# Squares of the tokens summed by ScalarE from a second, token-major load, and the in-projection's first two token tiles taken through the weights together

## The chip, the cores and the metric

One core of one Trainium2 chip runs the whole program. The metric is the device time of one execution in microseconds (us), the median of several runs.

## What is computed

The reference is one layer of a bidirectional encoder on two requests of 2048 and 256 tokens, in float32. The change lies in the first step of it, the normalized input projection of the attention heads and gates:

```
def rmsnorm(x, w):
    y = x * rsqrt(mean(x * x, axis=-1) + EPS)
    return y * w
...
h = rmsnorm(x, norm1_w)
p = h @ w_in            # split into mLSTM q,k,v,o; gates; attention q,k,v
m_out = mlstm_mixer(...)      # both directions, chunks of 64
a_out = attention_mixer(...)  # per-head RMS norm of q and k, rotary angles, softmax
x = x + concat(m_out, a_out) @ w_out
x = x + (silu(g) * a) @ w_down   # [a; g] = depthwise conv of rmsnorm(x) @ w_up
```

After it a final RMS norm. Each token has 1024 channels; the mean of their squares gives one factor `rc` per token.

## The kernel before

The 2304 tokens are 18 tiles of 128; tiles 16 and 17 are the short request and come first, then tiles 0 to 15 (`order`). A float32 product is made of three matmuls on split operands: a value is a rounded high part and a low remainder, and high·high, high·low and low·high are added (L260). `phase_a` handles the columns of `w_in` for attention and gates, 800 of them; the mLSTM's part, attention, out-projection and feed-forward follow later and are not touched.

For tile i of `phase_a`:

- `front_a` (L189) loads x channel-major: 128 channels on the partitions, 8 groups of channels by 128 tokens, 512 KB, into a buffer `x` (three of them; tiles 16 and 17 use buffers named `first`).
- `front_b` makes the high part on ScalarE (L196) and the low part on VectorE (L197) into `n1T` (three buffers) and stores both, 1 MB, for the later phases (L198).
- `front_c` squares x on ScalarE (L205, output `xq`), and GpSimd adds the 8 channel groups in three steps, 512, 256 and 128 elements per partition (L208 twice, L209, output `sq`).
- `front_d` sums the remaining 128 channels with a matmul against ones (L216, `rs_a`), adds EPS on VectorE (L218) and takes the power -1/2 on GpSimd (L219), which gives column i of `rc`.
- `mm` (L260) makes the projection `pj`: 8 chunks c of channels, two ranges of columns (512 and 288), three matmuls each, 48 matmuls per tile. Two `pj` buffers exist. Weights `w_a` are loaded and split per chunk in `weights` (L111, L112, L116).
- `post_a` scales `pj` by `rc` on ScalarE into `qk` (L269; two buffers), splits v, adds the gate bias (`gtm`, L278), squares q and k (L281), sums per head (`ms`, L283), and GpSimd makes the factors `rqk` (L104, L105).
- `post_b` on VectorE multiplies by `rqk` (L289), applies the rotary tables `tab` (L298, L302, L304) and splits into `kz` and `qz` (ScalarE L308, VectorE L309).
- `post2` transposes `kz` on TensorE (`pk`, L344) and stores it. `pg` (L337) are transposes of gates.

The rotary tables are multiplied with the head-norm weights once: two tiles' worth on VectorE and 28 small products on GpSimd (`tables2`, L247). During the first 8 tiles the weights of the mLSTM (`rm`, `wm`) are also loaded and split.

Each engine takes its instructions strictly in the order of its own stream. That order comes from a scheduler of the program's framework, which places instructions by priorities and a model of their times; a moved statement can so shift neighbours. DMAs issued from SyncE stand in SyncE's stream in the same way, so that one that waits for a free buffer holds those behind it.

Of the kernel before, what the change touches and what calls it, by code (L numbers as in the profile page):

```python
# [9 lines left out]
F32 = mybir.dt.float32  # L10
F32R = mybir.dt.float32r
AF = mybir.ActivationFunctionType
ALU = mybir.AluOpType
# [4 lines left out]
P = 128  # L18
D = 1024
NCC = D // P  # L20
T1, T2 = 2048, 256
T = T1 + T2
NT = T // P
# [4 lines left out]
EPS = 1e-6  # L28
# [125 lines left out]
def phase_a(g, tc, sw, st_x, after_x, after_mm, after_pj, wm):  # L154


    nc = g.nc
    with ExitStack() as st:
# [21 lines left out]
        xw = [first[k].rearrange("p (c t) -> p c t", c=NCC) for k in range(NX0)]  # L180

        xs = {}
        sqs = {}

        def front_a(i):

# [13 lines left out]

        def front_c(i):

            x = xs.pop(i)
            xq = sx.tile([P, NCC, P], F32, tag="xq", name=f"xq{i}", bufs=2)
            nc.scalar.activation(xq, x, AF.Square, scale=1.0 / 32.0)  # L205
            sq = sf.tile([P, P], F32, tag="sq", name=f"sq{i}")
            for k in (4, 2):
                nc.gpsimd.tensor_tensor(xq[:, 0:k], xq[:, 0:k], xq[:, k:2 * k], ALU.add)  # L208
            nc.gpsimd.tensor_tensor(sq, xq[:, 0], xq[:, 1], ALU.add)  # L209
            sqs[i] = sq  # L210

        def front_d(i):

            sq = sqs.pop(i)
            ps = pp.tile([P, 2], F32, tag="rs", name=f"rs_a{i}", bufs=2)
            nc.tensor.matmul(ps, sq, g.ones, start=True, stop=True)  # L216
            r = g.rc[:, i:i + 1]
            nc.vector.tensor_scalar(r, ps[:, 0:1], EPS, None, ALU.add)  # L218
            nc.gpsimd.tensor_tensor(r, r, g.mhalf[:, 0:1], ALU.pow)  # L219

        def weights(cs):
            for c in cs:
                r = first[NX0 + c] if NX0 + c < 8 else sx.tile([P, D], F32, tag="x", name=f"ra{c}", bufs=3)
                split(g, ws[c][:, 0, :], ws[c][:, 1, :], g.w_a[c], r[:, 0:800], g.n1w[:, c:c + 1])
# [25 lines left out]
        def mm(*tiles):  # L250

            pjs = [pj_.tile([P, 1024], F32, tag="pj", name=f"pj{i}", bufs=2) for i in tiles]
            cols = ((0, 512), (512, 800))
            if tiles[0] == order[0]:
                steps = [(t, z, c) for c in range(NCC) for t in range(len(tiles)) for z in cols]
            else:
                steps = [(0, z, c) for z in cols for c in range(NCC)]
            for t, (c0, c1), c in steps:
                for k, (a, b) in enumerate(((0, 0), (0, 1), (1, 0))):
                    nc.tensor.matmul(pjs[t][:, c0:c1], nTs[tiles[t]][:, c, a, :], ws[c][:, b, c0:c1],  # L260
                                     start=(c == 0 and k == 0), stop=(c == NCC - 1 and k == 2))
            for i in tiles:
                nTs.pop(i)
            return pjs
# [82 lines left out]

        front_a(order[0])
        front_b(order[0])
        weights(range(0, 3))  # L350
        front_a(order[1])
        front_c(order[0])
        weights(range(3, 6))
        front_b(order[1])
        front_a(order[2])
        weights(range(6, NCC))
        front_c(order[1])
        front_b(order[2])
        tables()
        front_d(order[0])  # L360
        front_c(order[2])
        tables2(slice(0, 2))
        front_a(order[3])
        prev = []
        steps = []
        for n, i in enumerate(order):
            pj, = mm(i)
            if n + 1 < NT:
                front_d(order[n + 1])
            if n > 1:  # L370
                post2(order[n - 2], prev.pop(0))
            if n == NT - 1:
# [1400 lines left out]
def layout(inputs):  # L1773
# [4 lines left out]
    def col(v):  # L1778
# [4 lines left out]
    w_m = np.concatenate([w_m[:LASTP], w_m[LASTP:][:, :, :, [1, 2, 0, 3]]], axis=0)  # L1783
    arrays = {
        "xT": x.reshape(NT, P, NCC, P).transpose(0, 3, 2, 1),
        "w_a": np.concatenate([w_in[:, ACOL + 32:ACOL + 800], w_in[:, ACOL:ACOL + 32]], axis=1).reshape(NCC, P, 800),
        "w_m": w_m.reshape(4, NCC, P, 512),
        "w_up": inputs["w_up"][0].reshape(NCC, P, 2 * NFC, P).transpose(2, 1, 0, 3),
# [26 lines left out]
```

## Time and profile before

| | us |
|---|---|
| median of 3 runs | 3365.33 (3363.44 to 3370.14) |
| the profiled execution | 3363.86 |
| its span in the trace | 3361.9 |
| TensorE busy in the span | 3262.6 |
| in-projection of `phase_a`, first to last matmul | 8.2 to about 205 |

The profile is one execution on the chip. Engines are PE (TensorE; PEld its weight loads), DVE (VectorE), ACT (ScalarE), POOL (GpSimd) and SP (SyncE). L12 is line 12 of the kernel; busy time excludes waiting. A row of the timeline gives start, duration, engine, line, operation, output and inputs, how many instructions were merged, and in brackets the idle time ahead of it with what ended it. A row of the table by stretches gives a stretch of the span, its length, the busy time and number of instructions of each engine, the clock granted to TensorE (1.00 is full), the mean busy share of the 16 DMA engines, and what they moved in GB/s.

### The profile page before, as it was taken

The numbers are of one execution on the slowest core, as the hardware profiler recorded it, in microseconds if no ns is written. First come the engines' busy times: TensorE is split into PE (matmuls) and PEld (weight loads), VectorE is DVE, ScalarE is ACT, GpSimd is POOL, SyncE is SP. The second block draws the span as 40 slices with busy tenths as digits, with TensorE's granted clock in tenths as the row PEclk, the third lists the DMA queues.
The fourth block names the chain that finished last, engine by engine and source line by source line (L and its number), as shares of the span: only waits on it lengthen the run. The fifth ranks groups of instructions, "written<-read, shape, count | busy, mean of one in ns | idle before, by whom it ended". The sixth has DMA issues, their size and how long they took to land. (4 is left out here: it accounts for less than half of the span.)

```text
span 3361.9 us, 57158 instructions
## 1 busy us (share of the span) xinstructions
PE 3262.6 (97%) x21366; PEld 3038.9 (90%) x21366; DVE 2399.9 (71%) x3721; ACT 1803.6 (54%) x3799; POOL 1355.2 (40%) x1710
## 2 busy tenths in 40 slices
PE   8899999999999999899999999999999999999998
PEld 6788888888888888788888999999999998999998
DVE  7866687777768778976765778978877776453573
ACT  5546666667666777655553544446555555323331
POOL 8653033213333323421245457744544442751112
PEclk9999999999999999999999999999999999999999
DMA  8665333343336444433347334424232223875563
GB/s 273 224 202 165 94 118 106 99 129 94 118 105 190 131 134 127 124 111 96 99 141 262 116 109 141 146 88 177 100 100 94 94 100 110 303 259 173 174 217 105
DMA packets 300636, 483.03 MB, mean 144 GB/s; under 512 B 36597, under 2 KB 186279, under 8 KB 300359
## 3 DMA queue, kind: packets, MB, share of 16 engines
q1 hardware_dynamic: 247543, 348.34, 32.7%
q0 software_dynamic: 36256, 121.60, 10.9%
q10 hardware_dynamic: 16560, 9.44, 0.9%
q8 instruction: 168, 2.75, 0.3%
q14 instruction: 109, 0.89, 0.1%
HBM read 337.37 MB, written 141.91 MB: 143 GB/s over the span
## 5 line engine op out<-in xcount | busy, mean ns | idle before, releaser
L634 DVE TENSOR_TENSOR pl<-ps,ph 128x512 fp32r<-128x512 f32 x520 | 353.9, 684 | 206.8 <-ACT ps L633 194.8
L1238 PE MATMUL pa<-nt,wut 128*128 128x290 f32 (+1 forms) x3168 | 447.0, 297 | 7.8 <-ACT u L1256 5.7
L632 ACT ACTIVATE ph<-ps 128x512 fp32r<-128x512 f32 x520 | 309.8, 596 | 248.7 <-PE ps L629 243.3
L1238 PEld LDWEIGHTS pa<-nt,wut 128*128 128x128 f32 x3168 | 431.1, 189 | 10.3 <-ACT u L1256 7.8
L603 DVE TENSOR_REDUCE mx<-px 128x1 f32<-128x512 f32 (+1 forms) x528 | 346.3, 673 | 94.3 <-PE px L602 92.2
L1348 DVE SCALAR_TENSOR_TENSOR y<-u,cw,y 128x1152 f32<-128x1152 f32 (+1 forms) x176 | 319.1, 1813 | 38.3 <-ACT yc L1346 17.3
L646 PE MATMUL pv<-ph,v 128*128 128x512 f32 (+1 forms) x1040 | 318.8, 401 | 0.8 <-ACT ph L632 0.3
L633 ACT ACTIVATE ps<-ps 128x512 f32<-128x512 f32 x520 | 310.2, 597 | 0.0
L1567 PE MATMUL et<-tet,wet 128*128 128x384 f32 x1584 | 279.0, 336 | 0.0
L1567 PEld LDWEIGHTS et<-tet,wet 128*128 128x128 f32 x1584 | 277.1, 188 | 0.0
L1081 PEld LDWEIGHTS po<-cmx,wo 128*128 128x128 f32 x1728 | 222.3, 192 | 9.7 <-DVE cmx L1069 1.5
L1081 PE MATMUL po<-cmx,wo 128*128 128x256 f32 x1728 | 226.4, 285 | 1.5 <-DVE cmx L1069 1.3
L1567 PE MATMUL e<-te,we 128*128 128x384 f32 x1188 | 213.5, 340 | 13.1 <-ACT te L1409 7.1
L1567 PEld LDWEIGHTS e<-te,we 128*128 128x128 f32 x1188 | 210.7, 190 | 14.5 <-ACT te L1409 7.3
L628 PE MATMUL ps<-qq,kk 128*128 128x512 f32 x520 | 214.9, 415 | 4.6 <-DVE mx L603 2.8
L602 PE MATMUL px<-kk,qq 128*128 128x512 f32 (+1 forms) x528 | 203.0, 412 | 4.1 <-DVE mx L603 2.4
L629 PE MATMUL ps<-qm,kl 65*128 65x512 f32 x520 | 205.9, 398 | 0.0
L792 PE MATMUL mj<-mn,wm 128*128 128x256 f32 x1296 | 197.9, 287 | 5.4 <-ACT og L808 3.4
L792 PEld LDWEIGHTS mj<-mn,wm 128*128 128x128 f32 x1296 | 182.7, 191 | 21.6 <-ACT og L808 3.8
L802 PEld LDWEIGHTS mv<-wm,mn 128*128 128x128 f32 x1296 | 183.1, 190 | 18.0 <-ACT qb L798 1.9
L802 PE MATMUL mv<-wm,mn 128*128 128x256 f32 x1296 | 196.9, 285 | 1.2 <-ACT qb L798 1.1
L646 PE MATMUL pv<-pl,v 128*128 128x512 f32 x520 | 191.6, 400 | 0.1
(310 smaller groups left out, 7244.9 us busy)
## 6 DMA issues: line engine op xcount, KB each, us to landing
mn<-n_d SPq DMA_DIRECT2D x216, 256.0 KB, 3.2
ru<-w_up SPq DMA_DIRECT2D x88, 512.0 KB, 3.6
a_d<-y POOLq DMA_DIRECT2D x88, 288.0 KB, 2.6
a_d<-tc POOLq DMA_DIRECT2D x66, 288.0 KB, 2.9
n_d<-n1T SPq DMA_DIRECT2D x18, 1024.0 KB, 5.3
dm<-nm_d POOLq DMA_DIRECT2D x72, 256.0 KB, 4.1
mjn<-n_d SPq DMA_DIRECT2D x72, 256.0 KB, 3.6
mvn<-n_d SPq DMA_DIRECT2D x72, 256.0 KB, 3.1
```

What stands on the lines that cost most here:

```text
L603: nc.vector.tensor_reduce(s.mx[:, t, z0:z0 + 1], ps[:, 0:w], AX.X, ALU.max)
L628: nc.tensor.matmul(ps, kk[:, kc:kc + P], s.qq[:, 0:N], start=True, stop=False)
L632: nc.scalar.activation(ph, ps, AF.Exp)
L633: nc.scalar.activation(ps, ps, AF.Exp)
L634: nc.vector.tensor_tensor(pl, ps, f32(ph), ALU.subtract)
L646: nc.tensor.matmul(s.pv[0:HD if k in (1, 3) else P, 0:N], v, p, start=(kp == 0 and k == 0), stop=(2 * kp + 2 == s.nk and k == 5))
L792: nc.tensor.matmul(pj[:, o], s.w[c][:, a, o * P:(o + 1) * P], nT[c][:, :, h, :], start=(c + o + k == 0), stop=(c == NCC - 1 and k == 2 and ...
L802: nc.tensor.matmul(pv[:, o], nT[c][:, o, a, :], s.w[c][:, h, 256:512], start=(c + o + k == 0), stop=(c == NCC - 1 and k == 2 and o == 1))
L1081: nc.tensor.matmul(po[:, o], wo[z // 2][c][:, a, n], mx[c][:, h, :], start=(c == 0 and k == 0), stop=(c == NCC - 1 and k == 2))
L1238: nc.tensor.matmul(p[:, z], w[:, aa, c, :], ops[k][:, c, bb, z * m:z * m + m], start=c == 0 and i == 0 and not add, stop=c == NCC // 2 - 1 ...
L1348: nc.vector.scalar_tensor_tensor(y[:, s:e], u[:, s + k:e + k], cw[:, k, jj:jj + 1], y[:, s:e], ALU.mult, ALU.add)
L1567: nc.tensor.matmul(ps[m // 2][:, m % 2], w[:, aa, m * P:(m + 1) * P], t[:, bb], start=p == 0 and n == 0, stop=p == NP - 1 and n == 2)
```

## The change

`front_c` no longer takes the channel-major x. It loads the tile once more from a second copy of the tokens, `xtok`, that lies token-major in memory (128 tokens on the partitions, 1024 channels, 512 KB), squares it on ScalarE and lets the same instruction add up the row, so that the sum lands directly in column i of `rc`; GpSimd adds EPS and takes the power. The three GpSimd additions, the matmul against ones and VectorE's addition of EPS are gone, and `front_d` with them. The copy is made on the host by a reshape of the input.

The first call of `mm` now takes tiles 16 and 17 together: chunk by chunk, with tile 17 two chunks behind tile 16. The loads at the start change order with it: one weight chunk, then x of tile 17, then the other weights.

```diff
         def front_c(i):
-            x = xs.pop(i)
-            xq = sx.tile([P, NCC, P], F32, tag="xq", name=f"xq{i}", bufs=2)
-            nc.scalar.activation(xq, x, AF.Square, scale=1.0 / 32.0)
-            sq = sf.tile([P, P], F32, tag="sq", name=f"sq{i}")
-            for k in (4, 2):
-                nc.gpsimd.tensor_tensor(xq[:, 0:k], xq[:, 0:k], xq[:, k:2 * k], ALU.add)
-            nc.gpsimd.tensor_tensor(sq, xq[:, 0], xq[:, 1], ALU.add)
-            sqs[i] = sq
-
-        def front_d(i):
-            sq = sqs.pop(i)
-            ps = pp.tile([P, 2], F32, tag="rs", name=f"rs_a{i}", bufs=2)
-            nc.tensor.matmul(ps, sq, g.ones, start=True, stop=True)
+            xs.pop(i)
+            xq = sx.tile([P, D], F32, tag="xq", name=f"xq{i}", bufs=2)
+            nc.sync.dma_start(xq, g.xtok[i])
             r = g.rc[:, i:i + 1]
-            nc.vector.tensor_scalar(r, ps[:, 0:1], EPS, None, ALU.add)
+            nc.scalar.activation(xq, xq, AF.Square, scale=1.0 / 32.0, accum_out=r)
+            nc.gpsimd.tensor_scalar(r, r, EPS, None, ALU.add)
             nc.gpsimd.tensor_tensor(r, r, g.mhalf[:, 0:1], ALU.pow)
...
             if tiles[0] == order[0]:
-                steps = [(t, z, c) for c in range(NCC) for t in range(len(tiles)) for z in cols]
+                steps = [(t, z, n - 2 * t) for n in range(NCC + 2) for t in range(2) if 0 <= n - 2 * t < NCC for z in cols]
...
         front_a(order[0])
         front_b(order[0])
-        weights(range(0, 3))
+        weights(range(0, 1))
         front_a(order[1])
-        front_c(order[0])
+        weights(range(1, 3))
+        front_b(order[1])
         weights(range(3, 6))
-        front_b(order[1])
         front_a(order[2])
         weights(range(6, NCC))
+        front_c(order[0])
+        front_b(order[2])
         front_c(order[1])
-        front_b(order[2])
         tables()
-        front_d(order[0])
         front_c(order[2])
...
-            pj, = mm(i)
-            if n + 1 < NT:
-                front_d(order[n + 1])
+            if n == 0:
+                pj, pj1 = mm(*order[0:2])
+            elif n == 1:
+                pj = pj1
+            else:
+                pj, = mm(i)
...
         "xT": x.reshape(NT, P, NCC, P).transpose(0, 3, 2, 1),
+        "xtok": x.reshape(NT, P, D),
```

What the scheduler makes of it is seen in three places. In the rows, numbers behind an underscore are buffers, and the digits in a name are the tile. Line numbers of the changed kernel are lower by 7 to 11.

TensorE at the start, before: the first projection instructions.

```order
L260 MATMUL pj16_282<-w_a0_178,n1T16_195 128x512 x3
L260 MATMUL pj16_282<-w_a0_178,n1T16_195 128x288 x3
L260 MATMUL pj16_282<-w_a1_179,n1T16_195 128x512
L216 MATMUL rs_a16_266<-ones_127,sq16_211 128x2
L260 MATMUL pj16_282<-w_a1_179,n1T16_195 128x512 x2
L260 MATMUL pj16_282<-w_a1_179,n1T16_195 128x288 x3
L260 MATMUL pj16_282<-w_a2_180,n1T16_195 128x512 x3
L260 MATMUL pj16_282<-w_a2_180,n1T16_195 128x288 x3
L260 MATMUL pj17_388<-w_a0_178,n1T17_224 128x512 x3
```

The same place in the changed kernel.

```order
L249 MATMUL pj16_275<-w_a0_178,n1T16_195 128x512 x3
L249 MATMUL pj16_275<-w_a0_178,n1T16_195 128x288 x3
L249 MATMUL pj17_276<-w_a0_178,n1T17_209 128x512 x2
L249 MATMUL pj16_275<-w_a1_179,n1T16_195 128x512
L249 MATMUL pj17_276<-w_a0_178,n1T17_209 128x512
L249 MATMUL pj17_276<-w_a0_178,n1T17_209 128x288 x3
L249 MATMUL pj17_276<-w_a1_179,n1T17_209 128x512
L249 MATMUL pj16_275<-w_a1_179,n1T16_195 128x512 x2
```

Before, the scheduler had already mixed the two tiles, but tile 17 came in only after chunk 2 of tile 16; now it comes in after chunk 0. The matmul against ones is gone from the stream.

GpSimd around the table products (`tab`), before: the factor `rqk` of tile 16 stands among the last of them.

```order
L247 TENSOR_TENSOR tab_173<-tab_173,qkw_171 128x2x64 x5
L247 TENSOR_TENSOR tab_173<-tab_173,rot_172 128x2x64 x2
L104 TENSOR_SCALAR rqk16_347<-ms10_16_345 128x10
L247 TENSOR_TENSOR tab_173<-tab_173,rot_172 128x2x64 x3
L219 TENSOR_TENSOR rc_129<-rc_129,mhalf_125 128x1
L247 TENSOR_TENSOR tab_173<-tab_173,rot_172 128x2x64 x2
L105 TENSOR_TENSOR rqk16_347<-rqk16_347,mhalf_125 128x10
L208 TENSOR_TENSOR xq1_354<-xq1_354 128x512
```

In the changed kernel it stands ahead of all 28, and the `rc` of tiles 0 and 1 behind them.

```order
L104 TENSOR_SCALAR rqk16_385<-ms10_16_383 128x10
L105 TENSOR_TENSOR rqk16_385<-rqk16_385,mhalf_125 128x10
L236 TENSOR_TENSOR tab_173<-tab_173,qkw_171 128x2x64 x7
L236 TENSOR_TENSOR tab_173<-tab_173,rot_172 128x2x64 x2
L236 TENSOR_TENSOR tab_173<-tab_173,qkw_171 128x2x64
L236 TENSOR_TENSOR tab_173<-tab_173,rot_172 128x2x64 x3
L236 TENSOR_TENSOR tab_173<-tab_173,qkw_171 128x2x64
L236 TENSOR_TENSOR tab_173<-tab_173,rot_172 128x2x64 x2
L236 TENSOR_TENSOR tab_173<-tab_173,qkw_171 128x2x64 x5
L236 TENSOR_TENSOR tab_173<-tab_173,rot_172 128x2x64 x7
L207 TENSOR_SCALAR rc_129<-rc_129 128x1
L208 TENSOR_TENSOR rc_129<-rc_129,mhalf_125 128x1
```

ScalarE's stream in the changed kernel, tiles 4 to 6: the squares of the new load (L206) stand ahead of the scaling of a projection (L258), and the wait for that load with them.

```order
L195 ACTIVATE n1T9_1215<-x9_1143 128x8x128
L297 ACTIVATE qz3_907<-t1_3_898 128x8x64
L206 ACTIVATE xq6_892,rc_129<-xq6_892 128x1024
L258 ACTIVATE qk6_1200<-pj6_1145,rc_129 128x800
L297 ACTIVATE kz4_1018<-t1_4_1008 128x2x64
L270 ACTIVATE qkq6_1208<-qk6_1200 128x640
L206 ACTIVATE xq7_1002,rc_129<-xq7_1002 128x1024
```

Before, the squares read the x that was loaded for the projection anyway, and ran ahead: those of tiles 5 and 6 stand beside the scaling of tile 1.

```order
L196 ACTIVATE n1T4_688<-x4_612 128x8x128
L112 ACTIVATE wm0_3_721<-rm0_3_0_722,nw_131 128x512
L205 ACTIVATE xq5_806<-x5_726 128x1024
L112 ACTIVATE wm0_4_843<-rm0_4_0_844,nw_131 128x512
L269 ACTIVATE qk1_673<-pj1_614,rc_129 128x800
L345 ACTIVATE kT16_551<-pk16_550 128x256
L205 ACTIVATE xq6_928<-x6_848 128x1024
```

So the square of tile 6 has moved from about five tiles ahead of its use to directly in front of it.

From about the end of `phase_a` on, the streams of both kernels are the same but for a few exchanged neighbours.

More of the change, by code (lines that the diff above doesn't have):

```diff
@@ L182, in phase_a @@
         xs = {}
-        sqs = {}
         def front_a(i):
```

## The prediction

> **What bounds the kernel now.** I read the page first. TensorE is busy for 97% of the span; the other 99 us (3361.9 less 3262.6) are all that can be won by filling gaps.
>
> ```profile
> span 3361.9 us, 57158 instructions
> PE 3262.6 (97%) x21366; PEld 3038.9 (90%) x21366; DVE 2399.9 (71%) x3721; ACT 1803.6 (54%) x3799; POOL 1355.2 (40%) x1710
> ```
>
> The change lies in the first 205 us, so I next cut these by stretches at the starts of tiles, which TensorE's timeline gives: tiles 16 and 17, then 0 and 1, 2 to 4, 5 to 8, 9 to 11, 12 to 15.
>
> ```profile
> core 0: us, PE busy (x) PEld busy (x) DVE busy (x) ACT busy (x) POOL busy (x), PEclk, DMA share, GB/s
> 8.22:30.45 22.23, 21.59 (x103) 18.59 (x103) 19.85 (x29) 12.70 (x16) 18.81 (x24) 1.00 1.01 332
> 30.45:51.62 21.17, 19.02 (x104) 16.65 (x102) 14.76 (x19) 9.02 (x12) 19.68 (x26) 0.96 0.93 317
> 51.62:92.19 40.57, 33.98 (x163) 28.73 (x164) 35.76 (x66) 24.61 (x43) 34.13 (x28) 0.85 0.68 216
> 92.19:137.08 44.89, 38.77 (x220) 33.14 (x220) 39.95 (x78) 23.95 (x46) 27.54 (x25) 1.00 0.65 211
> 137.08:167.62 30.54, 28.42 (x165) 24.97 (x164) 24.40 (x52) 18.66 (x36) 21.13 (x18) 1.00 0.72 233
> 167.62:204.73 37.11, 37.11 (x214) 32.59 (x211) 26.22 (x67) 17.38 (x38) 20.26 (x22) 1.00 0.69 232
> ```
>
> The last four tiles take 37.11 / 4 = 9.28 us each with TensorE never idle: that is its floor for a tile. Tiles 2 to 4 take 13.5 us each, 5 to 8 take 11.2, 9 to 11 take 10.2. In the third stretch TensorE is idle for 6.6 us and its granted clock is down to 0.85, so that even its busy time is stretched. VectorE is at 88 and 89% in the third and fourth stretches. Who holds TensorE, and who holds VectorE, the waits up to 205 us say (the VectorE and GpSimd rows from 40 and 30 us on):
>
> ```profile
> PE pk L344 <- DVE kz L309: 10.1, 8, 2.1
> PE rs_a L216 <- POOL sq L209: 4.0, 3, 2.2
> PE pg L337 <- ACT kT L345: 2.0, 1, 2.0
> DVE qk L289 <- POOL rqk L105: 26.8, 16, 3.2
> POOL rqk L104 <- DVE ms L283: 27.7, 12, 4.8
> ```
>
> TensorE waits for VectorE's `kz`; VectorE waits for GpSimd's `rqk`, and GpSimd for VectorE's `ms`. It is a loop of VectorE and GpSimd, and the squares' additions sit in it. One turn of it from the timeline:
>
> ```profile
> 153.27 3.98 POOL L208 TENSOR_TENSOR xq<-xq 128x512 f32<-128x512 f32 x2 [1.07 <-ACT xq L205]
> 155.15 0.81 DVE L283 TENSOR_REDUCE ms<-qkq 128x10 f32<-128x640 f32 x1
> 157.34 0.57 POOL L104 TENSOR_SCALAR rqk<-ms 128x10 f32<-128x10 f32 x1
> 158.00 1.99 POOL L105 TENSOR_TENSOR rqk<-rqk,mhalf 128x10 f32<-128x10 f32 x1
> 160.01 1.08 DVE L289 TENSOR_TENSOR qk<-qk,rqk 128x640 f32<-128x640 f32 x1 [2.21 <-POOL rqk L105]
> ```
>
> `ms` was ready at 155.96, but GpSimd was in its additions until 157.25, so `rqk` and VectorE came 1.3 us late. The additions also slow VectorE while they run: L289 takes 1.08 us here, and 1.91 beside an addition that starts at 42.75 us.
>
> ```profile
> 40.80 1.97 POOL L105 TENSOR_TENSOR rqk<-rqk,mhalf 128x10 f32<-128x10 f32 x1
> 42.75 5.91 POOL L208 TENSOR_TENSOR xq<-xq 128x512 f32<-128x512 f32 x4
> 42.80 1.91 DVE L289 TENSOR_TENSOR qk<-qk,rqk 128x640 f32<-128x640 f32 x1 [3.23 <-POOL rqk L105]
> 50.37 0.93 ACT L269 ACTIVATE qk<-pj,rc 128x800 f32<-128x800 f32 x1 [4.98 <-DVE t L321]
> 51.62 5.65 PE L260 MATMUL pj<-w_a,n1T 128*128 128x512 f32 x20
> ```
>
> These rows are also the stall ahead of tile 2: its `pj` buffer is freed by the scaling of tile 0 at 50.37, whose `qk` buffer is freed by the rotary products of tile 16, which wait for tile 16's `rqk`; that stood behind the table products on GpSimd until 42.77.
>
> **The change part by part.** What leaves and comes, from the groups up to 205 us (18 tiles):
>
> ```profile
> L208 POOL TENSOR_TENSOR xq<-xq 128x512 f32<-128x512 f32 (+1 forms) x36 | 46.5, 1299 | 11.4 <-ACT xq L205 10.6
> L105 POOL TENSOR_TENSOR rqk<-rqk,mhalf 128x10 f32<-128x10 f32 x17 | 36.6, 2155 | 1.1
> L219 POOL TENSOR_TENSOR rc<-rc,mhalf 128x1 f32<-128x1 f32 x18 | 20.7, 1152 | 18.1 <-DVE rc L218 18.1
> L104 POOL TENSOR_SCALAR rqk<-ms 128x10 f32<-128x10 f32 x17 | 12.8, 755 | 28.1 <-DVE ms L283 27.7
> L209 POOL TENSOR_TENSOR sq<-xq 128x128 f32<-128x128 f32 x18 | 11.4, 638 | 0.3
> L953 ACT ACTIVATION_READ_ACCUMULATOR s<-hh x144: 185/192/260, 439.9 to 1425.4; 128x1 f32 x144
> ```
>
> *GpSimd* loses (46.5 + 11.4) / 18 = 3.2 us per tile and gains one EPS addition, for which I take L104's 0.76 us. What stays, 0.76 + 0.76 + 1.15 + 2.16 = 4.8 us per tile, is half of a tile's time. *ScalarE* gains the reading of its accumulator, 0.19 us per tile (the median of a later line that does the same); it is busy for 106 of these 196 us, which hides it. If that cover were gone it would cost 18 x 0.19 = 3.4 us. *TensorE* loses the matmul against ones; from the row at 186.02 below to the next it holds TensorE for 0.14 us, so a tile's floor is 9.28 - 0.14 = 9.14.
>
> ```profile
> 186.02 0.28 PE L216 MATMUL rs_a<-ones,sq 128*128 128x2 f32 x2
> 186.16 0.34 PE L344 MATMUL pk<-identr,kz 128*128 128x128 f32 x2
> ```
>
> *The new loads* are 128 x 1024 x 4 B = 0.524 MB per tile. Tiles 2 to 4 move 216 GB/s x 40.57 us / 3 = 2.92 MB each, which becomes 3.45 MB; tiles 5 to 11 move 2.37 MB each, which becomes 2.89. The first two stretches show what a full queue moves, 332 and 317 GB/s: at those rates tiles 2 to 4 need 10.4 to 10.9 us each, and tiles 5 to 11 need 8.7 to 9.1, which TensorE's 9.14 covers. So the DMA becomes the bound of tiles 2 to 4, at 10.65. The Trainium skill, "DMA: Bandwidth & Descriptors", Specifications, gives some 358 GB/s as one core's limit to HBM. By it, as an estimate, those tiles could go at 9.6, and the sum below would gain 3 us more; the two full stretches here stay under it on average.
>
> On SyncE each load waits for its `xq` buffer, that is, for the square two tiles before, with the next store of `n1T` and the next x behind it. That square is done about two tiles before the new one is due, and x is loaded three tiles ahead, so I cost this at nothing; if the loads were later than that, it is the slow rival below.
>
> *Tiles 16 and 17.* The first stretch holds two tiles, 18.3 us at the floor, and takes 22.23. Chunk 0 now feeds 12 matmuls instead of 6 while the weights trickle in, but the DMA is full there (1.01), and the last weights come no earlier. I take 1.5 us of the 3.9; the ends are 0 and 3.9.
>
> *Tiles 0 and 1.* With `rqk` of tile 16 ahead of the tables, the stall before tile 2 should fall away. But x of tile 1 stands behind two new loads: 1.05 MB / 332 GB/s = 3.2 us later than the 34.1 at which ScalarE took it.
>
> ```profile
> 34.12 1.06 ACT L196 ACTIVATE n1T<-x 128x1024 fp32r<-128x1024 f32 x1 [1.39 <-DMA x<-xT]
> 35.21 1.23 DVE L197 TENSOR_TENSOR n1T<-x,n1T 128x1024 fp32r<-128x1024 f32 x1 [2.22 <-ACT n1T L196]
> ```
>
> So its parts are ready at 34.12 + 3.2 + 1.06 + 1.23 = 39.6, while tile 0 would end at 30.45 - 1.5 + 9.14 = 38.1. Tile 1 then ends at 39.6 + 9.14 = 48.8. The scaling of tile 0 needs two things more. One is the rotary products of tile 16, which by the old distance (42.80 to 50.37) end some 7.6 us after 39.6, at 47.2. The other is `rc` of tile 0, which now stands behind the 28 table products on GpSimd:
>
> ```profile
> 24.87 3.10 POOL L247 TENSOR_TENSOR tab<-tab,qkw 128x128 f32<-128x128 f32 x7 [1.31 <-DMA qkw<-k_norm_w]
> L247 POOL TENSOR_TENSOR tab<-tab,rot 128x128 f32<-128x128 f32 x14 | 8.5, 629 | 0.1
> L247 POOL TENSOR_TENSOR tab<-tab,qkw 128x128 f32<-128x128 f32 x14 | 6.4, 481 | 1.3 <-DMA qkw<-k_norm_w 1.3
> ```
>
> They take 14.9 us and start after tile 16's `rqk`, at about 30.5 instead of 24.87 (tile 16 done near 25, then scaling, squares, `ms` and L104, L105), so they end at 45.4 and `rc` follows 1.9 us later, at 47.3. With the scaling both are done by 48.2, just ahead of tile 1's end. So tile 2 starts at 48.8 instead of 51.62, both stretches together -2.8; ends: 0 and -6.8 (both at the floor).
>
> *Tiles 2 to 4* go at the DMA's 10.65: 32.0 instead of 40.57, -8.6. The TensorE wait for `sq` (4.0 us) is gone with its instruction, and without long gaps the clock should not fall to 0.85. *Tiles 5 to 11* are 75.43 us. The loop loses GpSimd's additions and what they cost VectorE; 9.14 is the floor and 10.18 (30.54 / 3) what tiles 9 to 11 show with the additions. I take 9.6, about midway, as VectorE's work (8.1 us per tile in tiles 9 to 11) plus the 2.6 us through L104 and L105 is only partly overlapped: 67.2, so -8.2. *Tiles 12 to 15* win 4 x 0.14 = 0.6. After the last tile, the changed stream has its `kz` transposes up to a tile later relative to the projections; matmuls of the mLSTM fill in there, and I charge 1.0 (0 to 4).
>
> Sum: -2.8 - 8.6 - 8.2 - 0.6 + 1.0 = -19.2. Against the profiled execution (3363.86, its span and 1.96 around it) that is 3344.7; the median of the runs shown lies 1.5 higher, so I expect 3346.
>
> **The rivals.**
>
> *TensorE alone paces (3338).* If the DMA serves the added loads without being the bound and the loop falls below the floor, tiles 2 to 11 take 91.4 instead of 116.0: -24.6, in all -2.8 - 24.6 - 0.6 + 1.0 = -27.0. For it: in the last stretch VectorE's work is 6.6 us per tile with hardly any additions left. Against it: the DMA's full stretches. The Trainium skill, "SBUF — State Buffer", Who interferes with whom, says that VectorE with two inputs in SBUF and a GpSimd operation that reads SBUF take turns, each blocked for the other's whole instruction; by that rule VectorE gets up to the whole 3.2 us per tile back, and the outcome is this one. The trace agrees in kind (1.08 against 1.91 us for L289).
>
> *The DMA backlog lasts (3354).* The start wins nothing because the queue is already full, tiles 2 to 4 go at 10.9 (-7.9), and 5 to 11 stay at 10.18 (71.3, -4.2): -7.9 - 4.2 - 0.6 + 1.0 = -11.7.
>
> *The loop stays (3359).* VectorE's own work and the way through L104 and L105 are the loop, and the additions were mostly waiting in its gaps: tiles 2 to 4 go at the 11.2 of tiles 5 to 8, later ones as before: -6.9 - 0.6 + 1.0 = -6.5. Against it speaks the turn at 155 us, where the additions are what is late.
>
> *Slower: ScalarE stands at the square.* In the new stream the square of tile 6 is directly ahead of the scaling of tile 6, and SyncE issues its load only after the store of `qz` of tile 1, which waits for VectorE. A load that lands late stops ScalarE, with the scaling, the next high part and `kz` behind it. Landing took this long for x in the first 120 us:
>
> ```profile
> DMA to landing us min/median/max: 6.6/6.9/8.8
> ```
>
> Nine pairs of tiles pass. If a pair loses d of TensorE's time, the gain of 19.2 is gone at d = 2.1, and at d = 4.5 the kernel is 21 us slower, 3387. Against it: with two `pj` buffers a scaling may come a tile late before TensorE stops, so a load must be some 9 us late to bite.
>
> **How the numbers follow.** A difference of 0.2% (6.7 us) is about what a measurement of this kernel can tell from none. Chances: the forecast 0.48, TensorE alone 0.17, the backlog 0.17, the loop 0.08, ScalarE at the square 0.10. Half of the loop's 0.08 and 0.04 of the last case lie within 0.2%: same 0.08, slower 0.06, faster 0.86. The range, 3337 to 3360, takes in the first four and leaves out the last and the open ends of the start and of the tail.
>
> **What would show it.** Right: the three groups of `rs_a`, `sq` and additions gone; L289's wait for L105 well under 26.8 us; the clock near 1.00 through 50 to 90 us; DMA share above 0.9 there; the last projection near 185 us. Wrong: `kz` waits still about 10 us (the loop), ScalarE waiting for `xq` loads with TensorE idle behind (the slow rival), or the time returned after 205 us, where the tail could take more than the 1 us charged.

## The result, and the profile after

The changed kernel takes 3354.75 us (median; 3351.51 to 3364.8), the kernel before, on the same chip, 3367.56 (3359.79 to 3374.12). The ratio is 0.9967, with a 95% interval from 0.9953 to 0.9981: 11 us faster, give or take 5. The profiled execution says the same, a span of 3349.8 us against 3361.9.

```profile
span 3349.8 us, 57072 instructions
PE 3256.3 (97%) x21330; PEld 3035.3 (91%) x21330; DVE 2367.5 (71%) x3703; ACT 1806.2 (54%) x3817; POOL 1292.7 (39%) x1674
```

GpSimd has lost 62 us of work and VectorE 32, far more than the time fell. The stretches of the changed kernel, again cut at the starts of tiles 16, 0, 2, 5, 9 and 12 and at the first matmul of the mLSTM:

```profile
core 0: us, PE busy (x) PEld busy (x) DVE busy (x) ACT busy (x) POOL busy (x), PEclk, DMA share, GB/s
7.50:28.11 20.61, 20.18 (x97) 17.25 (x98) 11.94 (x14) 13.04 (x16) 1.79 (x5) 1.00 1.06 362
28.11:50.69 22.58, 17.69 (x98) 15.32 (x97) 15.13 (x33) 9.65 (x15) 22.10 (x34) 1.00 1.06 384
50.69:79.56 28.87, 28.87 (x154) 25.13 (x155) 24.02 (x56) 19.97 (x38) 14.95 (x12) 0.94 0.99 351
79.56:118.67 39.11, 36.64 (x206) 31.65 (x204) 30.70 (x68) 24.71 (x48) 19.27 (x16) 1.00 0.96 308
118.67:149.79 31.12, 29.15 (x154) 25.12 (x155) 21.12 (x52) 19.58 (x39) 11.71 (x14) 0.95 0.89 295
149.79:186.81 37.02, 37.02 (x214) 32.50 (x213) 28.81 (x68) 24.64 (x53) 18.38 (x23) 1.00 0.76 247
```

Against the table of before, tiles 2 to 4 have become 11.7 us shorter (28.87 for 40.57) and tiles 5 to 8 shorter by 5.8; tiles 16 and 17 are 1.6 us shorter, tiles 0 and 1 1.4 longer, tiles 9 to 11 0.6 longer, and tiles 12 to 15 take as long as they did. The last projection ends at 187.0 us instead of 204.9. The waits up to 205 us show what is left:

```profile
POOL rc L207 <- ACT xq L206: 32.7, 8, 19.9
ACT qk L258 <- POOL rc L208: 15.9, 5, 8.8
DVE qk L278 <- POOL rqk L105: 13.6, 11, 2.5
PE pj L249 <- ACT qk L258: 9.3, 4, 4.9
PE mv L794 <- ACT qb L790: 3.3, 1, 3.3
```

TensorE's waits for `kz` (10.1 us) and `sq` (4.0) are gone. In their place it waits 9.3 us for the scaling (L258), and the scaling waits for `rc`. The largest of these waits, ahead of tile 2, from the timeline of all engines (PE: TensorE, POOL: GpSimd, ACT: ScalarE):

```profile
38.71 1.04 ACT L206 ACTIVATE xq<-xq 128x1024 f32<-128x1024 f32 x1
44.22 4.49 POOL L236 TENSOR_TENSOR tab<-tab,rot 128x128 f32<-128x128 f32 x7
49.11 0.57 POOL L208 TENSOR_TENSOR rc<-rc,mhalf 128x1 f32<-128x1 f32 x1
49.71 0.93 ACT L258 ACTIVATE qk<-pj,rc 128x800 f32<-128x800 f32 x1 [8.83 <-POOL rc L208]
50.69 1.65 PE L249 MATMUL pj<-w_a,n1T 128*128 128x512 f32 x3 [4.89 <-ACT qk L258]
```

TensorE was through with tile 1 at 45.8. The sum of squares of tile 0 had left ScalarE nine us before (first row), but `rc` stood behind the table products on GpSimd until 48.8. The three other waits, of 0.51, 1.96 and 1.96 us, stand at 107.10, 118.67 and 140.72, ahead of tiles 8, 9 and 11. At the first the scaling waits 3.47 us for `rc`, which stands behind `rqk` on GpSimd. The two longer ones come from ScalarE's order, here the last:

```profile
138.80 1.06 ACT L195 ACTIVATE n1T<-x 128x1024 fp32r<-128x1024 f32 x1 [2.52 <-PE pj L249]
139.76 0.91 ACT L258 ACTIVATE qk<-pj,rc 128x800 f32<-128x800 f32 x1
```

The high part `n1T` waits for a buffer that the running tile's last matmul frees, and the scaling of the tile before, which frees the next `pj`, stands behind it.

Of the 17.9 us that the in-projection won, not all arrives. At the first `mv` the changed kernel is 18.4 us ahead of before, 10 us later 14.6, and past 287 us of before only 8.0. Two waits, and the lower clock behind them, hold the loss:

```profile
196.87 4.03 PE L794 MATMUL mv<-wm,mn 128*128 128x256 f32 x19 [3.34 <-ACT qb L790]
...
259.88 1.01 PE L784 MATMUL mj<-mn,wm 128*128 128x256 f32 x3 [4.42 <-DMA mn<-n_d]
261.11 1.05 PE L784 MATMUL mj<-mn,wm 128*128 128x256 f32 x4
264.78 4.86 PE L794 MATMUL mv<-wm,mn 128*128 128x256 f32 x23 [0.70 <-ACT qb L790]
```

The same place in the kernel before:

```profile
271.28 0.62 PE L792 MATMUL mj<-mn,wm 128*128 128x256 f32 x3 [1.26 <-DMA mn<-n_d]
271.98 0.64 PE L792 MATMUL mj<-mn,wm 128*128 128x256 f32 x4
274.56 3.14 PE L802 MATMUL mv<-wm,mn 128*128 128x256 f32 x24 [0.89 <-ACT qb L798]
```

The wait for the `mn` load is 3.2 us longer, and behind it each matmul takes about 1.6 times as long (1.05 us for four instead of 0.64; 4.86 for 23 instead of 3.14 for 24). The granted clock of the two stretches behind 255 us, after first:

```profile
187.00:255.00 68.00, 60.09 (x449) 56.29 (x449) 41.75 (x85) 32.83 (x78) 38.46 (x99) 0.95 0.68 208
255.00:270.00 15.00, 9.88 (x46) 8.93 (x46) 5.40 (x9) 1.02 (x3) 5.63 (x11) 0.66 0.66 186
```

and before:

```profile
271.00:286.00 15.00, 13.83 (x106) 13.15 (x107) 7.55 (x16) 5.32 (x17) 7.89 (x17) 1.00 0.94 276
```

So TensorE does 46 matmuls there where it did 106: the wait and the clock that falls with it. The clock is the larger part. From the last projection to 287 us of before, the changed kernel's clock stands at half from 197.30 to 200.71, 217.78 to 221.19 and 258.74 to 268.98 us, with 15.2 us of matmuls in these stretches; before, it stands at half from 223.97 to 227.39, with 2.8 us of them. If a matmul there lasts twice as long as at the full clock, then by this estimate some 6 of the 10 us are slowed matmuls; the longer wait is 3.2.

### The profile page after: what moved, and what is told of

It reads as the page before. It is cut to its first block, busy times and chain, and to the rows that moved or that the text cites. A ratio compares the mean times of both kernels' runs of the same rounds, so it can differ in the third digit from the quotient of the medians.

```text
span 3349.8 us, 57072 instructions
## 1 busy us (share of the span) xinstructions
PE 3256.3 (97%) x21330; PEld 3035.3 (91%) x21330; DVE 2367.5 (71%) x3703; ACT 1806.2 (54%) x3817; POOL 1292.7 (39%) x1674
## 5 line engine op out<-in xcount | busy, mean ns | idle before, releaser
L1230 PEld LDWEIGHTS pa<-nt,wut 128*128 128x128 f32 x3168 | 432.8, 190 | 13.0 <-ACT u L1248 11.4
```

What stands on the lines that cost most here:

```text
L1230: nc.tensor.matmul(p[:, z], w[:, aa, c, :], ops[k][:, c, bb, z * m:z * m + m], start=c == 0 and i == 0 and not add, stop=c == NCC // 2 - 1 ...
```

## The experiments

My theory was that the additions on GpSimd, and the loop of VectorE and GpSimd in which they sat, were what the change took away, and the start order little. The rivals were the start, the way to `rc`, and the price of the added loads. e5, e9 and e10 leave out part of the sum of squares or take it over the wrong axis, so they do not compute the reference and serve for their times alone. The runs lie on several chips, and each ratio is to the kernel before on the same chip. The table stands ahead of the runs: median time; ratio to before with its interval; end of the last projection; and how far TensorE is ahead of the kernel before (us) at the first `mv` (215 us of before) and past the `mn` wait (287 us). Where the last two columns say "other order", the scheduler has laid out the mLSTM anew: of TensorE's first 4700 rows behind the in-projection 1200 to 1600 stand out of the order of before, against 132 or fewer in the other runs, so that no matmul there can be set beside its like.

| kernel | us | ratio | last projection ends | ahead at mv | ahead past mn |
|---|---|---|---|---|---|
| changed kernel | 3354.75 | 0.9967 (0.9953 to 0.9981) | 187.0 | 18.4 | 8.0 |
| e1 start only | 3362.47 | 0.9993 (0.9984 to 1.0001) | 202.7 | 1.9 | 2.2 |
| e2 squares only | 3357.15 | 0.9967 (0.9953 to 0.9980) | 185.2 | 20.0 | 9.6 |
| e3 additions kept | 3364.34 | 0.9989 (0.9980 to 0.9999) | 202.2 | -0.4 | -2.3 |
| e4 rc ahead | 3354.37 | 0.9965 (0.9953 to 0.9977) | 185.2 | other order | other order |
| e5 additions out | 3340.08 | 0.9917 (0.9905 to 0.9929) | 182.8 | 23.4 | 20.5 |
| e6 scaling first | 3353.82 | 0.9957 (0.9944 to 0.9969) | 180.8 | other order | other order |
| e7 in order | 3352.95 | 0.9953 (0.9941 to 0.9965) | 190.2 | 16.0 | 11.4 |
| e8 in order, third qk | 3354.14 | 0.9956 (0.9939 to 0.9972) | 189.4 | other order | other order |
| e9 no load | 3344.33 | 0.9929 (0.9915 to 0.9944) | 178.4 | 27.2 | 25.0 |
| e10 load unread | 3359.23 | 0.9975 (0.9965 to 0.9985) | 180.4 | other order | other order |
| e11 sums on TensorE | 3355.46 | 0.9960 (0.9945 to 0.9974) | 188.9 | 17.3 | 14.7 |
| e12 mixed | 3337.72 | 0.9910 (0.9894 to 0.9926) | 180.7 | 25.4 | 25.2 |

**The two parts apart.** e1 has the squares of before and the start of the change; e2 is the other half:

```diff
-                steps = [(t, z, n - 2 * t) for n in range(NCC + 2) for t in range(2) if 0 <= n - 2 * t < NCC for z in cols]
+                steps = [(t, z, c) for c in range(NCC) for t in range(len(tiles)) for z in cols]
...
-                pj, pj1 = mm(*order[0:2])
+            pj, = mm(i)
```

> The new order of the start with tiles 16 and 17 taken together; the squares as before (channel-major, three GpSimd additions, the matmul against ones). Theory (the GpSimd additions in the loop of VectorE and GpSimd are what tiles 2 to 11 lost): these tiles go as slowly as before, the last projection ends between 202 and 206 us (204.9 before, 187.0 in the changed kernel), TensorE's waits for kz stay near 10 us, and the time is within 3 us of before's. Rival (the gain comes from the start): the last projection ends at 192 us or earlier and the time is at least 8 us below before's.

> The squares by ScalarE from the token-major load, with the old order of the start. Theory (additions): tiles 2 to 11 go at some 9.6 us as in the changed kernel, the last projection ends between 187 and 190 us, and the time is 9 to 13 us below before's. Rival (start): the last projection ends at 198 us or later, and the time is within 5 us of before's.

Both came out on the side of the theory, with two misses: TensorE's waits for `kz` in e1 are 6.6 us and not near 10 (4.7 us at the scaling stand beside them), and e2 ends 2 us ahead of its range. The start alone moves the last projection by 2.2 us, and with the new squares it is worth nothing: e2 ends 1.8 us earlier without it, because there the table products start at 26.7 us, not 30.2, and `rc` of tile 0 follows them sooner (tile 2 starts at 47.9 us, not 50.7). All of the gain is the squares'.

**The additions put back (e3).** The changed kernel, and behind each square:

```diff
+            y = xq.rearrange("p (c t) -> p c t", c=NCC)
+            for k in (4, 2):
+                nc.gpsimd.tensor_tensor(y[:, 0:k], y[:, 0:k], y[:, k:2 * k], ALU.add)
+            sq = sf.tile([P, P], F32, tag="sq", name=f"sq{i}")
+            nc.gpsimd.tensor_tensor(sq, y[:, 0], y[:, 1], ALU.add)
```

> The changed kernel, with the three GpSimd additions done once more on each tile's squares into a buffer that nobody reads; the loads, the accumulator, and the way to rc are those of the change. Theory (the additions' time on GpSimd and beside VectorE is the cost): it gives back most of what the change won up to the last projection, which ends between 196 and 205 us, with VectorE waiting 20 us or more for rqk; the time is within 5 us of before's. Rival (what the change shortens is the way to rc, or the matmul in TensorE's stream, and not the additions): the last projection ends below 191 us and the time stays 8 us or more below before's.

The additions give back 15 us of the 18 (202.2 us), so they are the cost, but not in the way I had put it. Waits in e3 up to 205 us:

```profile
ACT qk L263 <- POOL rc L208: 25.1, 10, 5.0
DVE qk L283 <- POOL rqk L105: 13.1, 11, 2.3
PE pj L254 <- ACT qk L263: 12.2, 4, 6.5
PE pk L338 <- DVE kz L303: 6.4, 5, 3.0
```

VectorE waits 13.1 us for `rqk`, not the 20 expected. What grew is ScalarE's wait for `rc`, and VectorE's own rotary products, first in e3, then in the changed kernel:

```profile
L211 POOL TENSOR_TENSOR xq<-xq 128x512 f32<-128x512 f32 (+1 forms) x36 | 43.9, 1221 | 1.5
L213 POOL TENSOR_TENSOR sq<-xq 128x128 f32<-128x128 f32 x18 | 10.0, 557 | 1.0
L296 DVE TENSOR_TENSOR t<-qk,tab 128x256 f32<-128x256 f32 (+1 forms) x64 | 27.6, 473 | 0.0
```

```profile
L291 DVE TENSOR_TENSOR t<-qk,tab 128x256 f32<-128x256 f32 (+1 forms) x72 | 20.2, 335 | 0.1
```

Beside the additions one such product takes 473 ns instead of 335, 8.8 us in 64. Over all its rows up to the last projection VectorE is busy for 152.2 us in e3 and 131.9 in the changed kernel.

**The additions left out (e5).** The kernel before, with

```diff
-            sq = sf.tile([P, P], F32, tag="sq", name=f"sq{i}")
-            for k in (4, 2):
-                nc.gpsimd.tensor_tensor(xq[:, 0:k], xq[:, 0:k], xq[:, k:2 * k], ALU.add)
-            nc.gpsimd.tensor_tensor(sq, xq[:, 0], xq[:, 1], ALU.add)
-            sqs[i] = sq
+            sqs[i] = xq[:, 0]
```

> The kernel before, with the three GpSimd additions of each tile left out and nothing put in their place: the matmul against ones then sums only the first 128 of the 1024 channels, so the norm factors are those of a part of the channels. No token-major load, no accumulator, the old start. Theory (the additions are the whole cost, and the added loads and the accumulator cost nothing): the last projection ends between 183 and 188 us, as with the squares of the change (185.2 and 187.0), against 204.9; the time is 9 to 14 us below before's. If it is the loads or the squares' new place on ScalarE that hold the changed kernel back, this one ends at 181 us or earlier. Rival (the additions are hidden and something else of the change is the gain): the last projection ends at 197 us or later. On what is given back between 205 and 330 us: if a kernel that comes 18 us earlier to the mLSTM loads loses 6 to 8 us there whatever brought it there early, the wait for mn near 255 us (4.4 us in the changed kernel, 1.3 before) shows here too; if it comes from the changed kernel's own loads, it does not.

The end of the projection, 182.8, is 0.2 us ahead of the expected range; the time is well outside. It is 28 us below before, twice what the theory allowed, and more than twice what the change wins: the additions are worth 28 us, and the changed kernel loses some 15 of them again. Two waits of e5 up to 205 us:

```profile
DVE qk L285 <- POOL rqk L105: 27.4, 16, 2.8
PE pk L340 <- DVE kz L305: 2.5, 2, 1.6
```

VectorE waits as long for `rqk` as before (26.8), and the kernel is 28 us faster. That wait was never the cost. Between its first and last projection TensorE's idle time falls from 17.6 to 2.9 us (the wait for `kz` from 10.1 to 2.5, that for `sq` from 4.0 to none), and its busy time from 179.1 to 171.8, as the clock stays up (0.99 for 0.97). On what is given back: e5 is 23.4 us ahead at the first `mv`, further than the changed kernel, and keeps 20.5. So coming early is not by itself what costs there.

**The loads (e9, e10).** The changed kernel with the square on the x that is there anyway; e10 adds the load again, into a buffer of its own:

```diff
-            xs.pop(i)
-            xq = sx.tile([P, D], F32, tag="xq", name=f"xq{i}", bufs=2)
-            nc.sync.dma_start(xq, g.xtok[i])
+            x = xs.pop(i)
+            xq = sx.tile([P, NCC, P], F32, tag="xq", name=f"xq{i}", bufs=1)
+            nc.sync.dma_start(sx.tile([P, D], F32, tag="ld", name=f"ld{i}", bufs=1), g.xtok[i])
             r = g.rc[:, i:i + 1]
-            nc.scalar.activation(xq, xq, AF.Square, scale=1.0 / 32.0, accum_out=r)
+            nc.scalar.activation(xq, x, AF.Square, scale=1.0 / 32.0, accum_out=r)
```

> The changed kernel without the token-major loads: ScalarE squares the channel-major x that is there anyway, and its accumulator sums over the wrong axis, so the norm factors are those of channels and not of tokens. All else is the change's (accumulator, EPS on GpSimd, the paired start); the order of the instructions follows from the missing wait, with the squares well ahead. The kernel with the additions left out stands at 3340 us, the changed kernel at 3354. Theory (the loads cost the 14 us between the two, by their traffic or by tying rc to a late load): 3336 to 3343 us, last projection at 180 to 183 us, the wait for mn near 255 us at 3 us or less. Rival (what is left of the change, the start or GpSimd's EPS, or chance in the later stages, makes the 14 us): 3350 us or later.

> The kernel of the run before with the token-major loads put back, into a buffer that nobody reads: the DMA traffic of the change and its places in the queue of SyncE, without any engine waiting for it. The norm factors are again those of channels. If the traffic is the price of the loads: 3349 to 3356 us, as the changed kernel. If the tie is the price (rc that waits for a late square, behind the tables, ahead of the scaling): 3337 to 3344 us, as without the loads.

e9: 3344 us, 1 us above the expected range, last projection at 178.4, 1.6 ahead of it, and nearly all of it kept (25.0 us ahead past `mn`). So the accumulator, EPS on GpSimd and the start cost nothing that can be seen; the new loads do, 8.6 us up to the last projection (187.0 less 178.4). e10 tells what in them: with the same traffic, but no engine waiting for it, the projection ends at 180.4. The traffic itself is worth 2.0 us there, and 6.6 are the tie, `rc` that hangs on a square that hangs on the load. What costs is the place that the square and `rc` get by it, and not a load that lands late, for ScalarE waits for these loads only twice, both times ahead of 22 us:

```profile
ACT xq L206 <- DMA xq<-xtok: 3.2, 2, 3.0
```

The scaling, which waits 15.9 us for `rc` in the changed kernel, does not wait for it in e9 and e10. As the scheduler also orders other work of e10's in-projection otherwise (79 of ScalarE's 209 rows stand out of the order of the changed kernel), the 6.6 us are the price of the whole difference in order. The time of e10 (3359) would say the opposite, but it is lost after the projection, where its order is another; TensorE stands 8.2 us there:

```profile
PE gpt L445 <- DVE rows L408: 8.2, 1, 8.2
```

**The orders put right (e4, e6, e7, e8).** In e4 the table products stand behind the latest `rc`; in e6 `n1T` stands behind the scaling; e7 does both and also puts each square ahead of the scaling two tiles before; e8 adds a third `qk` buffer. The edits, all by an order that the scheduler has to keep; the first piece is e4's, the second e6's, the third is added in e7:

```diff
+                    with tc.issue_after(rcs[-1]):
+                        tables2(slice(2 * n + 2, min(2 * n + 4, NT1)))
...
+                    with tc.issue_after(sc[-1]):
+                        ins = front_b(order[n + 3]).ins
+                    behind.enter_context(tc.issue_after(ins))
...
+            with tc.issue_after(sqi[-1]) if n > 1 else ExitStack():
+                qk, r = post_a(i, pj)
```

> The changed kernel with each pair of table products on GpSimd held back until the latest rc of the stream is done, so that rc of tiles 0 and 1 stand ahead of the tables. Theory (the wait of 4.9 us ahead of tile 2 is rc of tile 0 standing behind the table products on GpSimd): tile 2 starts on TensorE between 45.5 and 47 us instead of 50.7, the last projection ends between 181 and 184 us instead of 187.0, and the time is 3 to 5 us below the changed kernel's if nothing later gives it back. Rival (x of tile 2, or the DMA that is full at that time, holds tile 2): tile 2 starts at 49 us or later and nothing is won. Second rival (the tables then come late for the rotary products): tile 2 starts early, but VectorE waits at the tables and the last projection ends above 185 us.

> The changed kernel, with the high part n1T of the tile three ahead held back on ScalarE until the scaling of the running tile is issued. Theory (the three stalls of 0.5, 2.0 and 2.0 us ahead of tiles 6, 7 and 9 are scalings that stand behind an n1T which waits for its buffer): these three go, the stall of 4.9 us ahead of tile 2 stays, and the last projection ends between 182 and 184 us instead of 187.0. Rival (the scaling is late through rc or its qk buffer anyway): stalls of the same size appear in other places, and the end is at 186 us or later. In time, at most 4 us below the changed kernel's, which these rounds can hardly tell.

> The changed kernel with three orders put right together: table products behind the latest rc on GpSimd, n1T behind the scaling on ScalarE, and the square of each tile ahead of the scaling of the tile two before. Theory (each stall of the in-projection is one of these three orders): TensorE has no wait of over 1 us for the scaling after tile 16, all tiles go at 9.2 to 9.4 us, and the last projection ends between 175 and 179 us. Rival (behind them stands the qk buffer, that is, VectorE's rotary products, as ScalarE's waits in the run with rc ahead show): the end is at 181 us or later, with ScalarE's scaling waiting for VectorE's t. In time: if 6 to 8 us are given back between 205 and 330 us as in the changed kernel, 3 to 9 us below the changed kernel's; if the giving back grows with the lead, the same as the changed kernel's.

> The kernel of the run before, with a third qk buffer (paid for by one kT buffer instead of two). If the qk buffer was what held the scaling there, the last projection ends 2 to 6 us earlier than without it, at 175 to 178 us; if not, within 1 us of it.

e4 shows that the stall ahead of tile 2 is `rc` behind the tables: tile 2 starts at 45.85 us without a wait. But a scaling that waits for its `qk` buffer stops TensorE for 4.8 us at 119, and the projection ends at 185.2, later than the 184 that the theory allowed. e6 shows that the two longer of the later stalls are ScalarE's order (one of 0.57 us is left, at 96.72): its end, 180.8, is below the 182 to 184 expected, since the stall ahead of tile 2 shrank as well, to 3.5 us. e7 missed. The scaling of tile 0, put behind the square of tile 2, came at 55.63 us (43.81 in e4), behind the post-processing of tile 17, and TensorE stood first at tile 17's `kz` and then at the scaling, from the timeline of e7:

```profile
45.71 0.29 PE L335 MATMUL pk<-identr,kz 128*128 128x128 f32 x2
53.19 0.49 PE L335 MATMUL pk<-identr,kz 128*128 128x128 f32 x2 [7.19 <-DVE kz L300]
56.59 1.65 PE L251 MATMUL pj<-w_a,n1T 128*128 128x512 f32 x3 [2.91 <-ACT qk L260]
```

Ten us are lost there at once; the other tiles go at 9.5 us. The third `qk` buffer gains 0.8 us, the second of the two expected cases. None of the four can be told from the changed kernel in time. What e4 and e6 win in the projection (1.8 and 6.2 us) does not show in the time, and in both the mLSTM is laid out anew; e10 loses time there too. That it is the layout that loses it is not shown; it was not tried by itself.

**The sums on TensorE (e11).** The kernel before, without additions and without the load:

```diff
-            nc.tensor.matmul(ps, sq, g.ones, start=True, stop=True)
+            for c in range(NCC):
+                nc.tensor.matmul(ps, sq[:, c], g.onesr, start=c == 0, stop=c == NCC - 1)
```

> The kernel before, with the three GpSimd additions replaced by TensorE: the squares are written in the rounded 32-bit type, and eight accumulating matmuls against ones take the place of one. No load, no accumulator, the old start; all of the reference is computed. If a matmul against ones costs TensorE 0.07 us (the row of two for 0.14 us, halved for the single pass), eight cost 0.56 us a tile in place of 0.14, 7.6 us in 18 tiles, so 3340 + 8 = 3348 us, and 6 us below the changed kernel. If each takes as long as a matmul of 128 columns (0.13 us), 16 us come on top and it is 3356 us or later, no better than the change.

3355 us: the worse of the two cases. The eight matmuls hold TensorE for 0.81 us (68.34 to 69.15), 0.10 us each, and the tiles go at 9.7 to 10.3 us:

```profile
68.34 0.95 PE L213 MATMUL rs_a<-onesr,xq 128*128 128x2 f32 x8
69.15 1.41 PE L257 MATMUL pj<-w_a,n1T 128*128 128x512 f32 x5
```

**A mixture (e12).** The first five tiles, where the tables and the full DMA made the load late, take their sums from TensorE; the other thirteen keep the change; and `n1T` stands behind the scaling, as in e6.

```diff
+            if order.index(i) < 5:
+                xq = sx.tile([P, NCC, P], F32R, tag="xq", name=f"xq{i}", bufs=2)
+                nc.scalar.activation(xq, x, AF.Square, scale=1.0 / 32.0)
...
+                for c in range(NCC):
+                    nc.tensor.matmul(ps, xq[:, c], g.onesr, start=c == 0, stop=c == NCC - 1)
```

> The changed kernel with three things: the first five tiles (16, 17, 0, 1, 2) take their sums of squares from TensorE, as in the run with eight matmuls, so that five of the eighteen token-major loads, those of the stretch in which the DMA is full, are gone; the other thirteen keep the token-major load; and n1T stands behind the scaling of the running tile, as in the sixth run. Theory (the loads cost by their traffic at the start and by tying rc to a late square behind the tables; the eight matmuls cost TensorE 0.9 us a tile, the 10.0 of that run less 9.1): tile 2 starts near 49 us without a stall of more than 1 us, the tiles after 2 go at 9.2 to 9.5 us, the last projection ends between 179 and 183 us. With the 3 to 4 us that such a lead gave back near 255 us, that is 3346 to 3351 us, below both kernels. Rival (thirteen loads still keep the DMA full enough): the end is at 185 us or later, and the time that of the changed kernel or above.

3337.7 us, ratio 0.9910 (0.9894 to 0.9926): below both kernels, 30 us under before and some 17 under the change. The projection ends where expected, though tile 2 starts at 52.4 us and not near 49; the time is below the expected 3346 because nothing is given back (25.4 us ahead at `mv`, 25.2 past `mn`). As e12 also has the `n1T` order of e6, the share of the five tiles alone is not shown. Three stretches of e12, tiles 2 to 4, 5 to 8 and 9 to 11:

```profile
52.44:79.97 27.53, 27.53 (x159) 24.12 (x157) 24.61 (x58) 20.23 (x39) 14.19 (x14) 1.00 1.06 385
79.97:116.43 36.46, 36.46 (x208) 32.09 (x207) 27.95 (x65) 26.01 (x50) 23.10 (x18) 1.00 1.02 347
116.43:143.81 27.38, 27.38 (x156) 24.01 (x155) 21.84 (x53) 16.51 (x35) 11.42 (x12) 1.00 0.99 333
```

and TensorE's four longest waits up to 300 us:

```profile
PE rs_a L209 <- ACT xq L206: 7.6, 1, 7.6
PE mj L796 <- ACT og L812: 3.4, 2, 2.6
PE mj L796 <- DMA mn<-n_d: 1.3, 1, 1.3
PE mv L806 <- ACT qb L802: 0.9, 1, 0.9
```

The first row is the wait for the first data at the start. From there to the last projection TensorE never stops, with the DMA full; no scaling is waited for, and the waits for `qb` and `mn` are as short as before the change.

## Why the prediction was right, and where not

The time lies in the range, 9 us above the point, and the direction and the cause (the squares, not the start) held. Up to the last projection the sum was near: -20.2 predicted (the -19.2 less the tail's +1.0), -17.9 measured. That is in part luck, for steps that came out 1.9, 3.0 and 0.5 us worse stand beside one that came out 3.1 us better. By its steps:

- *Tiles 16 to 1 (-2.8).* Measured -0.9. Tile 0 starts at 28.11, 2.3 us earlier than before (1.5 taken, ends 0 and 3.9). The step that failed is that x of tile 1 would stand behind the new loads and arrive at 37.3: ScalarE took it at 34.49, and TensorE had tile 1 done at 45.8. The forecast that `rc` of tile 0 follows the tables was right (done at 47.3 forecast, 49.7 measured, as the tables took 18.5 us and not 14.9), and so this wait, which I had hidden behind a late tile 1, lay open: 4.89 us.
- *Tiles 2 to 4 at the DMA's pace (-8.6).* Measured -11.7. The DMA was full (0.99), but moved 351 GB/s, and TensorE never waited in this stretch. The 332 and 317 GB/s, which I took for a full queue, are not the most that it moves: the changed kernel moves 384 GB/s in the stretch before, and e12 385 GB/s for 27.5 us. The Trainium skill, "DMA: Bandwidth & Descriptors", Specifications, gives some 358 GB/s as one core's limit; the traces do not agree, as these two stretches are above it.
- *Tiles 5 to 11 at 9.6 us (-8.2).* Measured -5.2: the stalls of 0.5, 2.0 and 2.0 us, the two longer ones in a place I had named (ScalarE's order around the scaling) but for the square and not for `n1T`, and 3.4 us at half the clock behind the second. In e12 these seven tiles take 63.8 us, 9.12 each, about the floor of 9.14 that I had worked out.
- *Tiles 12 to 15 (-0.6).* -0.1.
- *The tail (+1.0, 0 to 4).* This term was mis-sized most: 9.9 us are given back by 287 us of before, against bounds of 0 and 4. I had looked for the transposes of `kz` only; the wait for `qb` (3.3), the `mn` load (4.4) and the clock behind both were not in the sum. It is the sign of being wrong that I had listed last, time returned after 205 us. In the profiled execution some 4 us of that come back in later stages, for a reason that is not shown: with the order of before, e5 gains 5 us there and e11 loses 10. The measured total is -11 to -13.

The loop, as I read it from VectorE's wait for `rqk`, did not stand up: e5 has the same wait and is 28 us faster. What the additions cost is `rc` and VectorE's lengthened rows, and through them `kz` and the clock. VectorE's busy time up to the last projection falls from 161.1 to 131.9 us, 1.6 us per tile, half of the 3.2 that the additions took on GpSimd. The rival whose number came nearest, the DMA backlog (3354), had the wrong mechanism; the rival in which TensorE alone paces is what e12 shows: its tiles 2 to 11 take 91.4 us, the 91.4 of that rival. The slow rival, ScalarE standing at the square, did not come: ScalarE waits for the new loads 3.2 us in all. What came is that `rc` hangs on a square late in ScalarE's stream, at most 6.6 us.

Left open is why the `mn` load lands late (11.9 us after its issue, against 8.7 before and 8.8 in e12), though by their names the same loads stand around it. It is not the lead (e5, e9 and e12 are further ahead), and the same load takes 11.7 us in e9, where TensorE waits 2.9 us for it.

## What to carry to other kernels

Price a removed piece of work by leaving it out: here that showed 28 us, of which the change kept 11, and where the rest went could then be asked. A long wait of an engine that is not the bound (27 us for `rqk`) says nothing until the bounding engine is seen to wait for it. And when a sum is moved to a load, look at what its result now stands behind in each in-order queue: for five tiles of eighteen another way to the same sum, together with `n1T` behind the scaling, beat both kernels.

## What the runs showed of the hardware

- A gap of TensorE can be paid twice, as the granted clock may fall to half behind it, here for 3.41 us or two or three times as long (10.24 us behind the 4.42 us wait, which so cost 3.5 us more). The length of the gap alone does not decide it. In the changed kernel the clock is 0.50 from 118.79 to 122.20 us, behind a gap of 1.96 us, and 1.00 behind the next gap of the same length; the row of 23 matmuls from the tile's start then takes 7.16 and 5.63 us (first two rows). In e11 2.03 us were enough, and in e9 2.91 were not (last row). The Trainium skill, "TensorE: Matmul & The Clock Gate", Part 1, says that the clock is halved after at least one idle window of about 3.4 us; the length of the slow stretches fits such a window, but these shorter gaps do not agree.

```profile
118.67 7.16 PE L249 MATMUL pj<-w_a,n1T 128*128 128x512 f32 x23 [1.96 <-ACT qk L258]
140.72 5.63 PE L249 MATMUL pj<-w_a,n1T 128*128 128x512 f32 x23 [1.96 <-ACT qk L258]
246.53 0.74 PE L783 MATMUL mj<-mn,wm 128*128 128x256 f32 x4 [2.91 <-DMA mn<-n_d]
```

- Beside 54 us of GpSimd's additions in e3 VectorE's rotary products grow by 8.8 us and all its rows up to the last projection together by 20.4 (131.9 to 152.2): it is slowed, but by well under half of the time that these additions run.
